# A four-layer convolution and pooling trunk on eight cores: another scratch buffer for the short convolution, half-size weight blocks, and matmuls placed over the joints

## The chip, the cores and the metric

One Trainium2 chip, all eight cores. Two sequences of 4096 tokens are cut into eight pieces of 1024, and each core works alone on its piece plus 92 tokens of history; nothing is exchanged. The time of a run is that of its slowest core, in microseconds (us) on the device.

A run comes in one of two states. In a *slow* run the cores of one die (0 to 3 or 4 to 7), sometimes of both, have a lower granted TensorE clock (the share of full speed that the throttle lets through, 1.00 at most) and take longer. I use *undisturbed cores*: the cores of a fast run at its highest clock. In the kernel before they differ by 20 us (5170 to 5190 in its profile), and so do their waits for weights (47 us on core 6, 63 on core 0).

## The reference, cut to what matters

```python
def conv_mixers(h, ...):                       # even layers
    a_val, a_gate, b_x, b_c, b_b = jnp.split(h @ w_in, ...)        # 5 x 1024 columns
    a = a_val * sigmoid(a_gate)                                    # GLU
    a = causal_depthwise_conv(a, conv_a_w) + conv_a_b              # 31 taps
    a = silu(layernorm(a, ...))                                    # over 1024 channels
    bo = b_b * causal_depthwise_conv(b_c * b_x, conv_b_w)          # 3 taps
    return concat([a, bo]) @ w_out
def reference(x, ...):
    for layer in range(4):
        h = rmsnorm(x, norm_mix_g[layer])
        x = x + (conv_mixers(h, ...) if layer % 2 == 0 else pool_mixer(h, ...))
        h = rmsnorm(x, norm_mlp_g[layer])
        x = x + square(relu(h @ w1)) @ w2                          # 2048 -> 8192 -> 2048
    return rmsnorm(x, final_g)
```

## The kernel before

Channels lie on the 128 partitions; a *column* is 128 channels, so mixers A and B have eight columns each. Tokens are cut into three tiles of up to 372. The engines are PE (TensorE, the matmuls), DVE (VectorE), ACT (ScalarE), POOL (GpSimd) and SP (SyncE); PSUM is the memory that PE's results go to, and the kernel uses eight banks of it. A small list scheduler in the program orders the instructions of DVE, ACT, POOL and SP by modelled readiness and priority; PE keeps program order. What a buffer's name says decides the dependencies: an instruction that writes a buffer waits for all earlier readers of it.

The 31-tap convolution of an A column is split by taps (one product of the input, shifted, with one coefficient): DVE does 22 taps in an accumulator in PSUM, ACT makes nine products and POOL adds them into one accumulator `pacc` through two scratch buffers, `prod`. The three-tap convolution of a B column uses the same two:

```python
q = cnt["prod"] % 2                            # conv(j), 31 taps; once per tap of POOL's share
P.act(... out=prod[q][:, o0:T], in_=a[:, o0 + kk:T + kk], scale=col(wb + kk) ...)
P.pool(... out=pa, in0=pa, in1=prod[q][:, o0:T], op=ALU.add ...)
# ... cut
q = cnt["prod"] % 2                            # B_mm, the short convolution; same two buffers
P.act(... out=prod[q][:, o0:T], in_=pbuf[:, o0 + kk:T + kk] ...)
P.pool(... out=cv[:, o0:T], in0=cv[:, o0:T], in1=prod[q][:, o0:T], op=ALU.add ...)
for (lo, hi) in ot:                            # at once after it: PE's third projection
    mm_item(bk, *bv, ...)                      # and DVE's product with cv, which frees the bank
    P.dve(... out=cb[:, 8 + j, lo:hi], in0=pst(bk, hi - lo), in1=cv[:, lo:hi], op=ALU.mult ...)
```

The mixer's order, the start of the program, and the joints (places where PE needs a norm):

```python
A_mm(0); A_mm(1); B_mm(0); A_mm(2); B_mm(1); A_mm(3); B_mm(2); B_mm(3)   # two columns each
# ... half of the output projection (B), then
for (lo, hi) in ot:
    ln_tile(lo, hi)                            # LayerNorm, tile by tile, PE has nothing else
# ... the other half of the output projection (A)
for (lo, hi) in split(0):                      # start: squares, norm, normed x, then projections
    for c in range(KC):
        square(c, lo, hi, "dve")
    to_normed(C_GMIX)(lo, hi)
even_mixer(0, to_raw(C_GMLP))
for (lo, hi) in split(M0[0]):                  # norm ahead of each MLP
    rms_row(lo, hi)
mlp(0, ...)
```

## Time and profile before

| | before |
|---|---|
| three timed runs | 5814, 5924, 5990 us (median 5924.39) |
| profiled run (fast) | 5190.0 us, mean clock 0.961 |
| PE busy / idle in it | 4713 / 477 us |
| first MLP matmul of layer 0 | 714.6 us |

The prediction below shows the lines that it rests on. The busy time by stretch of the kernel before, from the first projection to the LayerNorm (columns: stretch, its length, then busy time and instructions of PE, PE's weight loads, DVE, ACT and POOL, then granted clock, DMA share, GB/s):

```profile
84.70:608.80 524.10, 382.20 (x2304) 228.81 (x2303) 318.90 (x320) 147.36 (x170) 205.64 (x104) 0.87 0.28 49
```

PE has work for 382 of 524 us, and no other engine is full either. Then PE's timeline from the LayerNorm to the MLP (start, length, engine, source line, and in brackets the idle time before it and what ended it), and one joint of an odd layer:

```profile
608.85 1.39 PE L361 MATMUL ps<-cb,ones 128*128 128x362 bf16 x8
...
654.04 51.56 PE L361 MATMUL ps<-cb,wr 128*128 128x362 bf16 x320 [7.68 <-ACT cb L576]
705.43 1.38 PE L403 MATMUL ps<-scr,onesf 128*128 128x362 f32 x4
710.71 1.54 PE L403 MATMUL ps<-scr,onesf 128*128 128x362 f32 x2 [3.90 <-POOL scr L397]
714.58 5.80 PE L361 MATMUL ps<-hb,wr 128*128 128x362 bf16 x19 [2.32 <-DMA wr<-w]
...
1739.11 3.91 PE L403 MATMUL ps<-scr,onesf 128*128 128x358 f32 x6 [10.91 <-POOL scr L397]
```

The LayerNorm's first matmul is at 608.85, the MLP's at 714.58. At the joint (1739.11) PE waits 10.9 us for POOL's sums of squares.

### The profile page before, as it was taken

Reading aid. Unit: us, or ns where it says so; the run is one execution under the profiler, and the core shown is the slowest. Engines: PE = TensorE matmul, PEld = TensorE weight load, DVE = VectorE, ACT = ScalarE, POOL = GpSimd, SP = SyncE. Lnnn points to the kernel's source line nnn. Section 1 sums busy time; section 2 is a strip of 40 time slices with the busy share of each in tenths; the row PEclk is TensorE's granted clock in tenths of the full one; section 3 lists DMA queues with packets and bytes.
Section 4 is the critical chain, followed back from the end, with each engine's and each line's share of the span. In section 5 each row is a group of like instructions: output and inputs, shape, how many; then the busy total and the mean of one; then the engine's idle time right before and its main releaser. Section 6 shows DMA issues by size and latency. Waiting matters only on the chain.

```text
span 5190.0 us, 80534 instructions; the slowest of 8 cores (5169.9 to 5190.0 us)
## 1 busy us (share of the span) xinstructions
PE 4713.3 (91%) x31214; PEld 3023.5 (58%) x31214; DVE 1883.0 (36%) x2944; ACT 1119.8 (22%) x1998; POOL 863.1 (17%) x845
## 2 busy tenths in 40 slices
PE   3477899999999899999984788999999989999998
PEld 1244556666665566666652455666666656666665
DVE  5855432222233422222359555322222352222235
ACT  2322340101015501010123224301010271011012
POOL 1543030000003300000036441200000140000003
PEclk9788999999999999999997899999999999999999
DMA  5133333443342344444421323344434424444443
GB/s 114 18 53 62 57 59 73 74 74 70 70 73 51 65 74 74 74 74 74 74 44 31 65 49 66 68 77 77 74 74 76 76 46 75 81 74 75 80 74 98
DMA packets 59991, 354.67 MB, mean 68 GB/s; under 512 B 6112, under 2 KB 18528, under 8 KB 19680
## 3 DMA queue, kind: packets, MB, share of 16 engines
q0 software_dynamic: 46224, 331.58, 35.2%
q1 hardware_dynamic: 13392, 17.93, 1.1%
q8 instruction: 255, 4.18, 0.3%
q14 instruction: 120, 0.98, 0.1%
HBM read 672.66 MB, written 8.39 MB: 131 GB/s over the span
## 4 chain that ended last, share of the span: by engine, by line
PE 83%; DVE 5%; DMA 4%; POOL 3%; issue 2%; ACT 2%; DVEq 0%; POOLq 0%; ACTq 0%; SPq 0%
PE ps L361 81%; POOL scr L485 3%; DMA wr<-w_in 3%; DVE ps L490 2%; PE ps L632 1%; DVE hb L415 1%; DMA xs<-x 1%; PE ps L675 1%; DVE xs L420 0%; DVE xs L794 0%; PE ps L403 0%; DVE scr L397 0%; ACT scr L395 0%; DMA wr<-w 0%; POOL scr L397 0%
## 5 line engine op out<-in xcount | busy, mean ns | idle before, releaser
L361 PE MATMUL ps<-hb,wr 128*128 128x358 bf16 (+7 forms) x13056 | 2018.9, 318 | 267.3 <-DVE cb L528 198.7
L361 PEld LDWEIGHTS ps<-hb,wr 128*128 128x128 bf16 x13056 | 1282.4, 98 | 1002.1 <-issue 302.1
L361 PE MATMUL ps<-cb,wr 128*128 128x362 bf16 (+6 forms) x10752 | 1626.9, 314 | 48.9 <-ACT cb L576 21.0
L361 PEld LDWEIGHTS ps<-cb,wr 128*128 128x128 bf16 x10752 | 1049.1, 98 | 622.5 <-issue 56.2
L420 DVE TENSOR_TENSOR xs<-ps,xs 128x362 f32<-128x362 f32 (+6 forms) x1152 | 602.2, 524 | 1418.4 <-PE ps L361 1418.2
L721 ACT ACTIVATE cb<-scr 128x362 bf16<-128x362 f32 (+6 forms) x768 | 380.8, 496 | 3067.8 <-DVE scr L718 3067.8
L718 DVE SCALAR_TENSOR_TENSOR scr<-ps,rstd 128x362 f32<-128x362 f32 (+6 forms) x768 | 402.5, 524 | 1426.4 <-PE ps L361 1426.4
L356 POOL DMA_DIRECT2D wr<-w x192 | 101.9, 531 | 2521.4 <-PE ps L361 2417.0
L361 PE MATMUL ps<-cb,scr 128*128 128x362 bf16 (+4 forms) x3072 | 463.9, 312 | 0.0
L361 PE MATMUL ps<-hb,scr 128*128 128x362 bf16 (+3 forms) x3072 | 463.2, 312 | 0.0
L490 DVE SCALAR_TENSOR_TENSOR ps<-scr,cst_sb,ps 128x1086 f32<-128x1086 f32 (+1 forms) x336 | 446.2, 1328 | 30.8 <-DVE ps L490 0.9
L361 PEld LDWEIGHTS ps<-cb,scr 128*128 128x128 bf16 x3072 | 298.4, 97 | 159.6
L361 PEld LDWEIGHTS ps<-hb,scr 128*128 128x128 bf16 x3072 | 298.4, 97 | 159.6
L397 POOL TENSOR_TENSOR scr<-scr 128x368 f32<-128x368 f32 (+7 forms) x360 | 314.1, 879 | 231.1 <-ACT scr L395 219.3
L485 POOL TENSOR_TENSOR scr<-scr 128x1086 f32<-128x1086 f32 (+1 forms) x128 | 312.2, 2439 | 227.1 <-ACT scr L476 112.0
L395 ACT ACTIVATE scr<-xs 128x362 f32<-128x362 f32 (+11 forms) x405 | 196.1, 491 | 90.2 <-DVE xs L420 67.4
L411 ACT ACTIVATE hb<-xs,cst_sb 128x362 bf16<-128x362 f32 (+6 forms) x288 | 169.5, 589 | 56.5 <-DVE xs L420 52.7
L482 ACT ACTIVATE scr<-scr,cst_sb 128x1086 f32<-128x1086 f32 (+1 forms) x128 | 150.8, 1180 | 132.2 <-POOL scr L485 129.2
L356 POOL DMA_DIRECT2D scr<-w x64 | 34.0, 531 | 842.9 <-PE ps L361 798.2
L403 PE MATMUL ps<-scr,onesf 128*128 128x358 f32 (+7 forms) x42 | 25.1, 722 | 135.7 <-DVE scr L397 79.9
L403 PEld LDWEIGHTS ps<-scr,onesf 128*128 128x128 f32 x42 | 10.0, 274 | 143.7 <-issue 142.9
L523 POOL TENSOR_TENSOR scr<-scr 128x1086 f32<-128x1086 f32 (+1 forms) x32 | 66.1, 2065 | 65.0 <-ACT scr L520 61.7
(61 smaller groups left out, 1024.1 us busy)
## 6 DMA issues: line engine op xcount, KB each, us to landing
wr<-w POOLq DMA_DIRECT2D x192, 1024.0 KB, 7.9
scr<-w POOLq DMA_DIRECT2D x64, 1024.0 KB, 7.9
wr<-w_in POOLq DMA_DIRECT2D x40, 1024.0 KB, 10.8
wr<-w_out POOLq DMA_DIRECT2D x16, 1024.0 KB, 8.2
xs<-x SPq DMA_DIRECT2D x12, 744.0 KB, 15.2
y<-xs SPq DMA_DIRECT2D x32, 171.0 KB, 2.4
wr<-pool_w POOLq DMA_DIRECT2D x8, 512.0 KB, 5.1
y<-xs SPq DMA_DIRECT2D x16, 170.0 KB, 2.2
```

The source lines that it names most:

```text
L356: P.dma("pool", lambda h: h.dma_start(out=wslot[s][:, 0:n], in_=src), wsem[s], [], wb, 128 * n * 4)
L361: fns = [(lambda h, i=i, l=l, r=r: h.matmul(pst(bk, w), lhsT=l, rhs=r, start=(i == 0), stop=(i == last))) for i, (l, r) in enumerate(parts)]
L395: P.act(w, lambda h: h.activation(out=t[:, 0:w], in_=xs[:, c, lo:hi], func=AF.Square), R(X[c], lo, hi), [tb], prio)
L397: f(w, lambda h: h.tensor_tensor(out=acc[:, lo:hi], in0=acc[:, lo:hi], in1=t[:, 0:w], op=ALU.add), [tb] + R(B_acc, lo, hi), R(B_acc, lo, h ...
L411: P.act(hi - lo, lambda h: h.activation(out=hb[:, c, lo:hi], in_=xs[:, c, lo:hi], func=AF.Identity, scale=col(gcol)), R(X[c], lo, hi) + [B ...
L420: P.dve(hi - lo, lambda h: h.tensor_tensor(out=xs[:, m, lo:hi], in0=pst(bk, hi - lo), in1=xs[:, m, lo:hi], op=ALU.add), [PS[bk]] + R(X[m], ...
L482: P.act(L, lambda h, kk=kk, q=q: h.activation(out=prod[q][:, o0:T], in_=a[:, o0 + kk:T + kk], func=AF.Identity, scale=col(wb + kk)), ab + ...
L485: P.pool(L, lambda h, q=q: h.tensor_tensor(out=pa, in0=pa, in1=prod[q][:, o0:T], op=ALU.add), R(B_prod[q], o0, T) + pb, pb, 2)
L490: P.dve(L + 90, lambda h, kk=kk: h.scalar_tensor_tensor(out=cacc, in0=a[:, o0 + kk:T + kk], scalar=col(wb + kk), in1=cacc, op0=ALU.mult, o ...
L523: P.pool(L, lambda h, q=q: h.tensor_tensor(out=cv[:, o0:T], in0=cv[:, o0:T], in1=prod[q][:, o0:T], op=ALU.add), R(B_prod[q], o0, T) + R(B_ ...
L718: P.dve(w, lambda h, bk=bk, w=w, t=t, lo=lo, hi=hi: h.scalar_tensor_tensor(out=t[:, 0:w], in0=pst(bk, w), scalar=0.0, in1=rstd[:, lo:hi], ...
L721: P.act(w, lambda h, w=w, t=t, f=f, lo=lo, hi=hi: h.activation(out=cb[:, f, lo:hi], in_=t[:, 0:w], func=AF.Square), [tb], R(C[f], lo, hi), 0)
```

## The change

Its intent is to fill PE's holes outside the MLPs. Six parts:

1. **Scratch.** The short convolution uses `rstd`, idle during the mixer, in place of `prod`.
2. **Order.** Its last projection and product (`B_last`) come a step after the first part (`B_first`); columns go one by one.
3. **Half blocks.** The input projection is loaded in blocks of one column, in six half slots.
4. **Taps.** POOL and ACT take 11 of the 31 taps (9 before); ACT also starts DVE's accumulator.
5. **Start.** PE multiplies x before it is normed (gain only); rstd is applied to the results.
6. **Joints and LayerNorm.** Half of the output projection lies between the LayerNorm's tiles; the first MLP matmuls come ahead of the norm's row; the last norm of a tile comes after the next tile's first matmuls.

The diff holds more: the scheduler's modelled costs of POOL's work and of DMA issues are lower, weight slots are taken in another order, and some priorities and one late load differ.

```diff
-CONVP = 9
+CONVP = 11
-    win_d = nc.dram_tensor("w_in", [2, 20, 128, SLOT], ...)
+    win_d = nc.dram_tensor("w_in", [2, 40, 128, HALF], ...)
 # ... cut: load_h, six half slots; column-wise glu; raw start (start0)
+                P.act(L, lambda h: h.activation(out=cacc, in_=a[:, o0:T], func=AF.Identity, scale=col(wb)), ...)
-                P.dve(L, lambda h: h.tensor_scalar(out=cacc, in0=a[:, o0:T], scalar1=col(wb), ...), ...)
 # short convolution
-                        P.act(... out=prod[q][:, o0:T], in_=pbuf[:, o0 + kk:T + kk] ...)
-                        P.pool(... in0=cv[:, o0:T], in1=prod[q][:, o0:T] ...)
+                    P.act(... out=rstd[:, a:b], in_=pbuf[:, a + kk:b + kk] ...)
+                    P.pool(... in0=cv[:, a:b], in1=rstd[:, a:b] ...)
+            for j in (2, 4, 6):
+                A_mm(j)
+                A_mm(j + 1)
+                B_last(j - 2)
+                B_first(j - 1)
+                B_last(j - 1)
+                B_first(j)
 # LayerNorm
-            for (lo, hi) in ot:
-                ln_tile(lo, hi)
+            w = load_w(wout_d[i, 1, 2], SLOT)
+            ln_tile(*ot[0])
+            out_b(2, *w, (0, 1))
+            ln_tile(*ot[1])
+            out_b(2, *w, (2, 3))
+            w = load_w(wout_d[i, 1, 3], SLOT)
+            ln_tile(*ot[2])
+            out_b(3, *w)
 # odd layers' joint
+                            bks = [[w1_mm(wv, wb, mi, lo, hi) for mi in range(2)] for (lo, hi) in tiles]
+                            for bk2, (lo, hi) in zip(bks, tiles):
+                                rms_row(lo, hi)
-        odd_mixer(1, to_raw(C_GMLP + KC))
+        odd_mixer(1, to_raw(C_GMLP + KC, prio=0))
```

## The prediction

> **What bounds the kernel now.** I read the table of cores first, then the PE's waits, then stretches of the timeline, then the busy time by stretch.
>
> ```profile
> core 0: 5190.0 us, clock 0.961
> ...
> die 0 (median of its cores): 5177.6 us, clock 0.961
> die 1 (median of its cores): 5177.5 us, clock 0.961
> ```
> Both dies are equal, so the profiled execution (5190 us) was undisturbed. The timed runs (5814 to 5990 us, median 5924) were not like it: they are 734 us longer at the median. I work out the change on the profile and carry it to the timed runs at the end.
>
> ```profile
> PE ps L361 <- DVE cb L528: 201.1, 8, 65.6
> PE ps L403 <- DVE scr L397: 79.9, 3, 42.6
> PE ps L361 <- DMA wr<-w_in: 63.4, 19, 6.5
> PE ps L403 <- POOL scr L397: 55.8, 10, 10.9
> PE ps L361 <- ACT cb L576: 21.0, 3, 7.7
> PE ps L361 <- DVE cb L581: 19.5, 2, 9.8
> ```
> These are what TensorE (PE) waits for: total, times, longest. They sum to 441 us, nearly all of the 477 us in which PE is idle (5190 less 4713 busy). Line 528 is the last product of the short convolution, 397 the sum of squares of a norm, 576 and 581 the LayerNorm's output.
>
> ```profile
> core 0: us, PE busy (x) PEld busy (x) DVE busy (x) ACT busy (x) POOL busy (x), PEclk, DMA share, GB/s
> 0.00:84.70 84.70, 4.77 (x7) 1.81 (x8) 45.38 (x84) 24.33 (x51) 2.48 (x8) 1.00 0.62 152
> 178.00:256.00 78.00, 12.70 (x82) 7.71 (x80) 71.58 (x56) 25.14 (x22) 45.92 (x19) 0.61 0.00 0
> 256.00:504.00 248.00, 185.28 (x1088) 109.12 (x1088) 149.85 (x140) 73.05 (x78) 108.17 (x56) 0.88 0.32 57
> 614.00:654.00 40.00, 16.55 (x80) 8.81 (x78) 35.67 (x67) 28.04 (x45) 4.13 (x2) 0.72 0.07 15
> 714.00:1663.00 949.00, 945.95 (x6144) 594.55 (x6144) 232.44 (x433) 144.58 (x288) 73.95 (x108) 1.00 0.38 69
> ```
> The stretches are: start and first norm; the hole of the first even mixer; the rest of its projections; its LayerNorm; the first MLP. The MLP is full (946 of 949 us), so only the mixers, their joints and the two ends can give anything. The MLP also gives the price of a matmul: 945.95/6144 = 154.0 ns at 362 columns. In the 256-504 stretch no engine is full: DVE 60%, POOL 44%. So this is a chain of waits, not a full engine.
>
> ```profile
> 247.00 2.48 POOL L485 TENSOR_TENSOR scr<-scr 128x1086 f32<-128x1086 f32 x1 [0.20 <-POOL scr L485]
> 249.43 2.12 POOL L523 TENSOR_TENSOR scr<-scr 128x1086 f32<-128x1086 f32 x1
> ...
> 256.25 19.11 PE L361 MATMUL ps<-hb,wr 128*128 128x372 bf16 x112 [65.56 <-DVE cb L528]
> ```
> This is the largest wait. The first short convolution's POOL add (L523) stands after 32 adds of the long convolutions (L485, four convolutions of eight), because both use the two `prod` buffers in program order. PE has queued the products that need it, runs out of its five PSUM banks, and waits 65.6 us, later 19 and 19 (62, 16, 17 in layer 2).
>
> [...] the trace shows 0.61 and 0.88 granted in the stretches with holes, 1.00 in the MLP, so closing a hole also warms the matmuls after it. [...]
>
> **The change part by part.** Matmul counts of the projections do not change.
>
> *Start of layer 0.* Before, PE's first projection matmul is at 84.5 us: all x tiles and three 2.1 MB weight blocks (fp32 as read) share the DMA, the first x lands at 29.4 us, and each tile is squared, summed, normalised and scaled before PE starts. After, matmuls run on gain-scaled x and rstd is applied to their results; only one pair of half blocks (2.1 MB) precedes tile 0. The DMA delivered about 7.5 MB as read in the first 26 us (4.3 MB as written, of which 3.15 MB of weights count double), so some 290 GB/s. Tile 0 with its weights and constants (5.5 MB) is then in by about 21 us. Sixteen fp32 sums of squares on PE at 0.7 (warm, 1.38 for two at 705 us) to 1.6 us (cold, at 43 us) end near 35 us. The third pair of halves may land only near 55 us and hold PE some 10 us. The first block (two A columns and one C·x column, three tiles: 288 matmuls at 157.5 ns = 45 us) therefore ends near 97 us.
>
> *Middle.* Short convolutions use rstd as scratch, not `prod`, and their last product is emitted one step later (B_last), so that it is ready. I tested each engine on one pair of columns in layer 0. PE: 480 matmuls x 157.5 = 75.6 us. DVE: two convolutions of 19 taps (11 now go to ACT and POOL, one to ACT) and a last add, 40 x 1.457 (cadence of L490) = 58, plus 18 evacuations at 0.6 = 69 us; with 23 operations per convolution it would have been 78. POOL: 20 adds x 2.69 = 54, four short adds x 2.3 = 9, ten half loads at 0.55 = 68 us. ACT: 24 x 1.2 + 6 x 1.2 + 12 x 0.5 = 42 us. So PE is the bound, narrowly. The one accumulator of POOL makes a serial chain per convolution: first product 1.5 + ten adds 27 + loads and short adds between 7 + final DVE add 2 = 37.5 us, 75 us a pair: equal to PE. I leave 10 us of stall where the fourth column needs the first of three A buffers, 5 us at the end of the last convolution, 5 us for loads and cold clocks: 20 us of the 165 us of waits now between 84 and 654 us.
>
> *LayerNorm.* Its three tiles cost 23.5 us of PE waits (9.8, 6.0, 7.7). After, 192 matmuls of the other output half (29 us) are spread between and after them, and a tile's DVE chain is some 12 us, so they are hidden; DVE does 36 + 13 us in a stretch of 37 us and runs over by about as much as the second half of the projection gives.
>
> *Sum of layer 0*, to the first MLP matmul (714.6 us): 97 + 1632 x 157.5 ns (257) + 816 x 153.3 ns (125) + 20 + three norm matmuls 4.5 = 504. Saved: 210.
>
> *Layer 2*, from 2636.4 to 3282.9 (646.5 us): last two tiles of the MLP 39, projections 1920 x 151.7 = 291, output half and LayerNorm 816 x 147.5 = 120, six norm matmuls 9, waits 23: 482. Saved: 164. This holds the deferred norm of each tile, whose waits (5.3 and 7.0 us) go away.
>
> *Odd mixers.* Each ends with a wait for the squares (10.9 and 10.3 us). After, six groups of the MLP (14.8 us) come first: 20 saved. *End:* the finishes of tiles 0 and 1 move behind the next tile's first matmuls: 2.3 + 5.9 = 8 saved; the last 15 us stay.
>
> Together 210 + 164 + 20 + 8 = 402, so about 4790 us in the state of the profile, 0.92 of before.
>
> **Rivals.** *POOL becomes the bound.* It goes from 8 to 10 adds per convolution, gets the squares and rstd products of the start and twice as many loads, and stands in order: a load that waits for its slot holds up all adds behind it (POOL's waits for PE before a load are its longest). For it: 75 us of chain against 75.6 of PE, with nothing to spare. Against: half slots come free in half the time. If each of the eight convolutions ran 4 us late, each even layer would lose 30 us and the time in the profile's state would be 4850. *The clock takes it back.* [...] In the extreme nothing is gained (5900). Against: the clock was 1.00 throughout the full MLPs, so density alone did not throttle this execution. *Raw start fails.* If x tile 0 still lands near 30 us behind the weights, or the squares come in late, the first block ends near 120 us: 25 us lost, no sign changed. *The loads were the wait* (63 us on w_in): halves double the issues, but 1 MB landed in 8 to 11 us and half of it should take no longer, so I don't expect these waits to grow.
>
> **Range and chances.** In the timed runs PE is slower. Idle time that is removed does not scale, which gives 5924 - 402 = 5522. But the projections of the even layers, now dense (about 870 us of PE work), would stretch like the MLPs, by 16 to 23% or 140 to 200 us, of which the holes of the kernel before absorbed perhaps half: 70 to 100 us given back. At a slow clock POOL and DVE have slack, so the 20 us stalls shrink. I take 5580, a ratio of 0.942. The range 5400 to 5730 holds a mostly unthrottled spell at one end[...]. Faster by over 2%: 0.94; within: 0.05; slower: 0.01.
>
> **What would show it.** The first projection matmul near 35 us and the first full-width POOL add of a long convolution near 85; no PE wait over 12 us between 100 and 500 us; waits for the short convolution's product gone from 201 to under 20; granted clock over 0.95 there; the first MLP starting near 505; the LayerNorm's waits gone; MLP stretches unchanged to 1%. Wrong would be: PE waiting for the GLU products behind L516/L519 (the POOL chain), a first block that ends after 120 us, or MLPs at a lower clock than in before's run of the same state.

## The result, and the profile after

| | before | after |
|---|---|---|
| all runs up to the result | 15: median 5695, 5189 to 5996 | 14: median 4896, 4852 to 5649 |
| fast runs | from 5188.67 | seven, 4852 to 4862 |
| ratio of fast runs | | 0.9325 (95%: 0.9282 to 0.9368) |

A ratio here is the mean time of one kernel's fast runs over that of the other's fast runs of the same rounds, so it is not quite the ratio of medians or of profiled times. The change is faster by 6.7%. The predicted 5580 us, range 5400 to 5730, does not hold the measured 4896. That median is itself no typical run: it lies halfway between the slowest of seven fast runs (4862) and the fastest of seven slow ones (4931).

The profile recorded with the result fell in the slow state (first fence: its table of cores); a fast one (second fence) is the run called `a_same` below.

```profile
core 0: 5107.3 us, clock 0.924
...
core 4: 5503.8 us, clock 0.850
```

```profile
core 0: 4859.6 us, clock 0.980
core 1: 4860.2 us, clock 0.979
core 2: 4829.3 us, clock 0.987
...
core 4: 4832.6 us, clock 0.985
...
core 6: 4859.7 us, clock 0.979
```

Even in the fast run some pairs of cores (0 and 1, 6 and 7) end 27 us after the others. From about 2890 to 3050 us, around the start of MLP 2 (2925), their clock is 0.81. Two cores in the same 104 us:

```profile
core 1: us, PE busy (x) PEld busy (x) DVE busy (x) ACT busy (x) POOL busy (x), PEclk, DMA share, GB/s
2936.00:3040.00 104.00, 104.00 (x581) 63.51 (x580) 25.27 (x39) 21.79 (x43) 5.26 (x9) 0.81 0.39 62
...
core 2: us, PE busy (x) PEld busy (x) DVE busy (x) ACT busy (x) POOL busy (x), PEclk, DMA share, GB/s
2936.00:3040.00 104.00, 104.00 (x707) 68.60 (x706) 28.02 (x48) 23.90 (x49) 3.73 (x7) 1.00 0.39 72
```

Both are full of matmuls, but one gets through 581 and the other 707. So I compare stages on core 4, which has no dip. What PE waits for there (total, times, longest):

```profile
PE ps L372 <- DMA wr<-w_in: 14.8, 4, 11.3
PE ps L414 <- POOL scr L408: 14.3, 5, 4.2
PE ps L372 <- DVE cb L567: 14.2, 8, 3.3
PE ps L372 <- ACT cb L640: 13.5, 2, 7.0
PE ps L887 <- ACT scr L884: 13.3, 1, 13.3
PE ps L372 <- DVE scr L480: 10.9, 1, 10.9
```

Line 567 is now the short convolution's product: 14.2 us, against 201.1 before. Line 414 is the norm's row (55.8 before for POOL's squares), line 640 the LayerNorm's output, line 480 the GLU's product. The busy time by stretch: start and first block; rest of the projections; LayerNorm and output projection; first MLP.

```profile
core 4: us, PE busy (x) PEld busy (x) DVE busy (x) ACT busy (x) POOL busy (x), PEclk, DMA share, GB/s
0.00:114.00 114.00, 76.21 (x383) 42.79 (x384) 66.17 (x120) 45.42 (x78) 54.17 (x61) 0.90 0.64 140
114.00:412.00 298.00, 279.68 (x1778) 171.59 (x1776) 253.70 (x247) 158.79 (x181) 249.90 (x132) 0.98 0.45 66
412.00:523.00 111.00, 99.46 (x615) 60.85 (x614) 70.51 (x132) 71.08 (x129) 42.43 (x49) 0.92 0.42 66
523.00:1471.00 948.00, 945.10 (x6152) 594.25 (x6149) 238.39 (x436) 148.88 (x296) 77.54 (x112) 1.00 0.45 70
```

In the second row PE is at 94%, DVE at 85% and POOL at 84% of 298 us, at a clock of 0.98; before, PE had 73% (382.2 of 524.1) at 0.87. A matmul takes 157.3 ns here (279.68/1778), before 165.9 (382.20/2304). The MLP is unchanged: 945 us of matmuls. The stages side by side:

| stage | before | after | gain | predicted gain |
|---|---|---|---|---|
| start to layer 0's first MLP matmul | 714.6 | 523.05 | 191.5 | 210 |
| layer 0's MLP | 948.9 | 948.0 | 1 | 0 |
| layer 2: end of tile 0 of MLP 1 to MLP 2's first matmul | 649.0 | 482.0 | 167 | 164 |
| two odd joints | 94.1 + 92.5 | 94.8 + 92.2 | 0 | 20 |
| end | 68.2 | 68.2 | 0 | 8 |
| whole, undisturbed core | 5190.0 | 4832.6 | 357 | 402 |

The odd joints run from the mixer's first matmul to the end of the norm; the 96 MLP matmuls that now lie inside (14.8 and 14.2 us) are added on the side of before. The column before is its core 0, the slowest of eight cores that end between 5170 and 5190 us, so some 10 us of the 357 are a matter of which core one takes.

### The profile page after: what moved, and what is told of

It is laid out like the page before. It is cut to its first block, busy times and chain, and to the rows that moved or that the text cites. A ratio compares the mean times of both kernels' runs of the same rounds, so it can differ in the third digit from the quotient of the medians.

```text
span 5503.8 us, 80816 instructions; the slowest of 8 cores (5106.2 to 5503.8 us)
## 1 busy us (share of the span) xinstructions
PE 5371.3 (98%) x31236; PEld 3273.2 (59%) x31244; DVE 1815.7 (33%) x2905; ACT 1185.4 (22%) x2067; POOL 1014.8 (18%) x967
## 4 chain that ended last, share of the span: by engine, by line
PE 95%; DVE 2%; issue 1%; POOL 1%; ACT 0%; DMA 0%; SPq 0%; DVEq 0%; POOLq 0%; ACTq 0%
PE ps L372 92%; PE ps L703 1%; DVE ps L516 1%; PE ps L746 1%; DMA xs<-x 0%; POOL scr L880 0%; SPq L395 0%; DVE xs L752 0%; PE ps L414 0%; POOL scr L513 0%; POOL scr L550 0%; PE ps L676 0%; DVE xs L908 0%; DVE rstd L423 0%; DVE hb L437 0%
## 5 line engine op out<-in xcount | busy, mean ns | idle before, releaser
L372 PE MATMUL ps<-hb,wr 128*128 128x358 bf16 (+7 forms) x13056 | 2268.4, 344 | 46.2 <-ACT scr L879 11.6
L372 PEld LDWEIGHTS ps<-hb,wr 128*128 128x128 bf16 x13056 | 1374.9, 105 | 935.1 <-issue 62.3
L372 PE MATMUL ps<-cb,wr 128*128 128x362 bf16 (+6 forms) x10752 | 1866.7, 344 | 25.9 <-ACT cb L640 13.7
L372 PEld LDWEIGHTS ps<-cb,wr 128*128 128x128 bf16 x10752 | 1137.1, 106 | 748.2 <-issue 31.7
L372 PE MATMUL ps<-cb,scr 128*128 128x362 bf16 (+4 forms) x3072 | 540.9, 346 | 0.0
L372 PE MATMUL ps<-hb,scr 128*128 128x362 bf16 (+3 forms) x3072 | 537.9, 345 | 0.0
L406 ACT ACTIVATE scr<-xs 128x368 f32<-128x368 f32 (+7 forms) x360 | 171.7, 486 | 89.6 <-DVE xs L442 80.3
L703 PE MATMUL ps<-wr,hb 128*128 128x512 bf16 x280 | 79.9, 453 | 1.6 <-issue 0.9
L550 POOL TENSOR_TENSOR scr<-scr,rstd 128x1086 f32<-128x1086 f32 (+6 forms) x40 | 79.6, 1992 | 6.3 <-ACT rstd L547 4.2
L423 DVE RECIPROCAL rstd<-scr 128x358 f32<-128x358 f32 (+7 forms) x21 | 49.5, 2361 | 78.7 <-ACT scr L421 78.7
```

Source lines behind the costliest of these rows:

```text
L372: fns = [(lambda h, i=i, l=l, r=r: h.matmul(pst(bk, w), lhsT=l, rhs=r, start=(i == 0), stop=(i == last))) for i, (l, r) in enumerate(parts)]
L406: P.act(w, lambda h: h.activation(out=t[:, 0:w], in_=xs[:, c, lo:hi], func=AF.Square), R(X[c], lo, hi), [tb], prio)
L703: fns = [(lambda h, k=k, bk=bk, lo=lo, hi=hi, m=m: h.matmul(ps[0:m, bk * 512:(bk + 1) * 512], lhsT=hb[:, 4 * g + k, lo:hi], rhs=wv[:, k * ...
```

## The experiments

Thirteen runs follow, eleven edited kernels and the changed kernel twice, all correct. The theory: nearly all of the gain comes from the short convolution's wait, and the prediction's size went wrong only because it took the slow state for the usual one. Rivals: the gain comes from the start, the order, or the half blocks; or a denser kernel is throttled more. The record's verdict on the first three edits (scratch alone, `prod` back, no deferral) is "unclear", and three edits have too few fast runs for any; what follows rests on undisturbed cores and on the waits. The kernels were not all run on the same chip; the kernel before reads alike on all of them (5164 to 5194), and the changed kernel on two (4829 to 4836).

**The changed kernel again (`a_same`, and later `a_again`).** No edit.

> The changed kernel once more, for a trace in the fast state. Fast runs 4850 to 4865 us, ratio to the kernel before 0.93 to 0.94. Theory A (the chain of the short convolution was the main wait): PE's waits for the short convolution's product fall from 201 us to under 30 over both even layers, and the first MLP starts between 515 and 530 us instead of 714.6. Theory B (the weight loads were the main wait) would show PE waits for w_in gone (63 us before) but the product's waits still over 60 us. On the states: if slow runs come with the chip and not with the kernel, this kernel has slow runs about as often as the kernel before in these rounds; if a denser TensorE is throttled more, it has clearly more.

> The changed kernel on the same chip as the three runs before, for comparison: fast runs 4850 to 4865 us, undisturbed dies 4835 to 4850.

*Measured.* `a_same`: one fast run of five, 4861.7 us, others 5105 to 5715; no ratio. `a_again`: fast runs 4859 to 4863, ratio 0.936 (0.9342 to 0.9379); undisturbed cores 4829 to 4836. 15 of 26 runs of the changed kernel were slow; of the kernel before, 16 of 32 in the experiments and at least 9 of the 15 with the result. So a denser kernel is not in the slow state notably more often, and outside the short dips its MLPs stay at 1.00 in the fast state. The rival "the clock takes it back" finds no support here.

**The kernel before, with the short convolution's scratch alone changed.**

```diff
-  P.act(... out=prod[q][:, o0:T] ...);  P.pool(... in1=prod[q][:, o0:T] ...)
+  P.act(... out=rstd[:, o0:T] ...);     P.pool(... in1=rstd[:, o0:T] ...)
```

> The kernel before with one thing of the change: the short convolution's products go into rstd's buffer in place of the two prod buffers. Theory A: its POOL adds no longer stand behind 32 long-convolution adds, PE's waits for the product fall from 201 to under 80 us, and the time from 5190 to about 5070 (fast). Rival: the long convolution itself (three A buffers, 23 DVE steps of 1.46 us, 40 to 50 us per column behind the projections) takes its place as the wait, the time stays within 60 us of 5190.

*Measured.* 4999.8, 5000.4 and 5037.4 us in its fast runs, ratio to before 0.9637 (0.9576 to 0.9698); undisturbed cores 4978 to 4998, some 190 us below before. Its PE waits:

```profile
PE ps L403 <- DVE scr L397: 80.0, 3, 42.7
PE ps L361 <- DMA wr<-w_in: 65.7, 19, 7.1
PE ps L403 <- POOL scr L397: 57.9, 10, 13.5
...
PE ps L361 <- DVE cb L526: 14.4, 8, 4.8
```

The product's wait falls from 201.1 to 14.4 (line 526 here, 528 before), and the time by the same 190; the other waits stand as they were. One buffer's name gives over half of the whole gain.

**The changed kernel, with `prod` back.**

```diff
-  P.act(... out=rstd[:, a:b] ...);     P.pool(... in1=rstd[:, a:b] ...)
+  P.act(... out=prod[q][:, a:b] ...);  P.pool(... in1=prod[q][:, a:b] ...)
```

> The changed kernel with the scratch put back to the two prod buffers, all else kept (later last product, half slots, new start). Theory A: the waits for the product come back in part (20 adds stand ahead in place of 32, and the product is used 30 us of PE later), 60 us per even layer, about 4970 us. Rival (the later product alone is enough, the scratch does nothing): under 4880 us.

*Measured.* 5051 to 5077 us, ratio 0.9742 (0.9695 to 0.9789); undisturbed cores 5044 to 5050, so 210 us lost.

```profile
PE ps L372 <- DVE cb L569: 214.1, 8, 41.3
```

The wait is back whole (line 569 is the product), although `B_last` is deferred here. So the scratch alone gives 190 us, and without it 210 of some 345 are lost; the deferral does not hide a wait of this size.

**No deferral.**

```diff
             short_conv(0)
+            B_last(0)
             for j in (2, 4, 6):
                 A_mm(j)
                 A_mm(j + 1)
-                B_last(j - 2)
                 B_first(j - 1)
                 B_last(j - 1)
                 B_first(j)
-            B_last(6)
+                B_last(j)
```

> The changed kernel with each column's last product emitted right after its own C.x product, all else kept. Theory A: each of eight products per layer waits for three ACT passes and two POOL adds (some 10 us, less what the five banks buffer), 40 us per layer, about 4930 us. Rival (the free scratch alone is enough): within 15 us of 4853.

*Measured.* Fast runs 4848.5 to 4899.7 us, ratio 0.9371 (0.9277 to 0.9465); undisturbed cores 4840 to 4851: some 10 us lost. The product's wait is 26.3 in 13 instead of 14.2 in 8. My expectation of a large loss was a miss: with scratch of its own the short convolution is ready soon, and the deferral has little left to hide.

**LayerNorm not interleaved.**

```diff
-            w = load_w(wout_d[i, 1, 2], SLOT)
-            ln_tile(*ot[0]) ... out_b(3, *w)
+            out_b(2, *load_w(wout_d[i, 1, 2], SLOT))
+            out_b(3, *load_w(wout_d[i, 1, 3], SLOT))
+            for lo, hi in ot:
+                ln_tile(lo, hi)
```

> The changed kernel with the three LayerNorm tiles after all of the first output half, as in the kernel before, all else kept. The changed kernel still waits about 11 us per even layer in its LayerNorm (4.5 and 7.2 us) against 23.5 before, so if the interleaving is worth only the difference, this is 25 us slower: fast runs near 4878. If it is worth the whole LayerNorm as my prediction had it, 45 to 50 us slower: 4900.

*Measured.* 4893 to 4913 us, ratio 0.9434 (0.9393 to 0.9476); undisturbed cores 4872 to 4877: 40 us lost, two layers together.

```profile
PE ps L372 <- ACT cb L640: 61.9, 6, 16.9
```

The LayerNorm's wait is 61.9 in six instead of 13.5 in two: the interleaving does its work.

**The start of before, all else changed.**

```diff
-        even_mixer(0, to_raw(C_GMLP), start0)
+        for (lo, hi) in split(0):
+            for c in range(KC):
+                square(c, lo, hi, "dve")
+            to_normed(C_GMIX)(lo, hi)
+        even_mixer(0, to_raw(C_GMLP), lambda n, lo, hi: None)
```

> The changed kernel with the start of the kernel before: each x tile squared, summed and normalised before PE's first projection matmul at about 84.5 us, all else kept. By the traces the first block of 288 matmuls ends at 113 us in the changed kernel; here it would end at 84.5 + 45 = 130. So 15 to 20 us slower: fast runs near 4870. Rival (the raw start is worth the 58 us by which the first projection matmul came earlier): 4910.

*Measured.* 4842.5 to 4869.3 us, ratio 0.935 (0.9302 to 0.9397); undisturbed cores 4836 to 4841. The raw start, the longest part of the diff, is worth about 5 us, although PE's first projection comes at 26.5 us with it and at 78.1 without (84.7 in the kernel before). (The expectation's 113 us is a misreading: counted in the next fence, the first block's 288 matmuls end at about 105.) Where the gain stops is in the PE timeline of the changed kernel (core 4, second run of the same):

```profile
26.50 5.21 PE L372 MATMUL ps<-hb,wr 128*128 128x372 bf16 x32
...
50.80 6.47 PE L372 MATMUL ps<-hb,wr 128*128 128x372 bf16 x32 [11.26 <-DMA wr<-w_in]
...
102.22 32.92 PE L372 MATMUL ps<-hb,wr 128*128 128x372 bf16 x208 [0.97 <-DVE scr L473]
146.05 14.16 PE L372 MATMUL ps<-hb,wr 128*128 128x362 bf16 x81 [10.91 <-DVE scr L480]
...
410.42 1.39 PE L372 MATMUL ps<-cb,ones 128*128 128x362 bf16 x8 [2.80 <-DVE cb L519]
```

With the old start the LayerNorm's first matmul is 5.6 us later (core 0 of that run):

```profile
416.01 1.39 PE L372 MATMUL ps<-cb,ones 128*128 128x362 bf16 x8
```

Two chains of nearly the same length end there. With the old start PE sets the time: it is busy for 326 of the 332 us between 78.1 and 410.5. With the raw start PE is ahead and gives the time back, in the wait of 10.9 us for a free A buffer (line 480) and in 2.8 at the end, and the chain of convolutions sets the time: its eight column adds (line 519) lie 37.5 us apart on average, from 146.6 to 409.0 us. That chain does not begin sooner. DVE's first step of a long convolution is at 117.1 us with the raw start and at 116.4 with the old one, its last add at 409.0 and 410.6.

The timeline and kernel.py tell why, though no run tests it. The first column's input is there at 102.2 us, when ACT forms the first product from it, but the accumulator on DVE's side lies in the PSUM banks (5 to 7) in which the raw start keeps its copies of rstd, and DVE's normed tiles read these until 114.3; ACT opens the accumulator at 115.9. It is the shared scratch over again, in a new place.

**Nine taps in place of eleven.**

```diff
-CONVP = 11
+CONVP = 9
```

> The changed kernel with 9 in place of 11 taps of the long convolution on ACT and POOL. Theory A: DVE then needs 22 operations of 1.457 us per column, 75 us a pair with the evacuations, as much as PE, and stalls come: 10 to 30 us slower in all, 4865 to 4885. Rival (POOL's serial chain was the tighter one, and it is relieved): not slower, 4840 to 4855.

*Measured.* One fast run of four, 4910 us with a disturbed pair, so no ratio; undisturbed cores 4852 to 4864: 20 to 25 us lost. PE's wait for the column add (line 519) grows from 2.8 to this:

```profile
PE ps L372 <- DVE cb L519: 30.6, 2, 15.5
```

That fits the chain as the bound: with nine taps DVE's half of it is the longer one. In layer 0 the column add waits for POOL in five of eight columns with eleven taps and in none with nine, where DVE does the last nine steps of the last column back to back.

**Joints of before.** Norm rows ahead of the MLP, gains at the old priority, last norm not deferred.

```diff
+            for (lo, hi) in tiles:
+                rms_row(lo, hi)
-                    if gi == 0 and blk == 0:
+                    if False:
-                                if late and (blk, mi) == (0, 2):
-                                    late()
 # ... cut
+                        by_tile(lo, hi)
-        odd_mixer(1, to_raw(C_GMLP + KC, prio=0))
+        odd_mixer(1, to_raw(C_GMLP + KC))
```

> The changed kernel with all joints as before: norm rows ahead of the MLP's first matmuls, gains of the odd mixers at the old priority, tiles finished at once and not behind the next tile's first matmuls. By the stretches of the two traces the new joints gain nothing at the odd mixers and nothing at the end, some 6 us at each even mixer's end and some 10 us before layer 2: 20 to 25 us slower, 4875. Rival (my prediction: 20 at the odd mixers, 8 at the end, besides those): 50 us slower, 4905.

*Measured.* Two fast runs (4934.5, 4935.6), both with dips, too few for a ratio; undisturbed cores 4862 to 4866: 31 us lost.

```profile
PE ps L414 <- POOL scr L408: 56.9, 10, 12.2
```

The parts together are worth 31 us, but not where I put them: against this run's core 3, the changed kernel gains about 5 and 4 us at the ends of the even mixers, 13 before layer 2 and 4 at the end. At the odd joints the stage table shows no gain:

```profile
1538.33 16.28 PE L372 MATMUL ps<-hb,wr 128*128 128x358 bf16 x96 [2.53 <-ACT hb L428]
1557.79 2.47 PE L414 MATMUL ps<-scr,onesf 128*128 128x358 f32 x4 [3.17 <-POOL scr L408]
1564.56 1.52 PE L414 MATMUL ps<-scr,onesf 128*128 128x354 f32 x2 [4.30 <-DVE scr L788]
```

The one wait of 10.9 us has become three, 2.5, 3.2 and 4.3, with 96 matmuls between at 16.3 us, where 96 at the first MLP's 154.0 ns would take 14.8. With the joints of before, the norm's first matmul comes 75 to 77 us after the start of layer 1's mixer (cores 2 and 3); here 86.7. So the new order itself brings the squares some 10 us later, and the matmuls put ahead hide nothing. That the gains, now first in ACT's order, push the squares back is likely, but not separated from the rest. The third wait is of the order's own making: six MLP groups and three norms want nine of eight PSUM banks, and the third norm waits for DVE to empty one.

**Half slots four deep, not six.**

```diff
+            if cnt["h"] > 6:                   # a load also waits for the readers of the next two slots
+                more = W[(s + 1) % 6].r + W[(s + 2) % 6].r
+                P.ops[n].deps = sorted(set(P.ops[n].deps) | set(more))
```

> The changed kernel with each half-block load of the input projection held back until the two next older half slots are free too, so that four half slots work in place of six; nothing else changes. If the finer and earlier loads are a part of the gain (PE's waits for w_in are 63 to 66 us in the kernels with whole slots and 14 in the changed one), these waits come back to over 40 us and the time rises by 30 or more, 4885. If the order of the short convolution is all, the time stays within 10 us of 4853 and the waits for w_in under 25 us.

*Measured.* One fast run, 4864.9, no ratio; undisturbed cores 4829 to 4836, as with six. PE's waits for w_in are 17.6 us on core 6 (14.8 with six). Depth past four is worth nothing here.

**Odd joints: every second gain on DVE.**

```diff
-                gain(c, lo, hi, gbase + c, prio)
+                (gain_dve if prio == 0 and c % 2 else gain)(c, lo, hi, gbase + c, prio)   # tensor_scalar
```

> The changed kernel with every second gain of the odd mixers on DVE (0.41 us) in place of ACT (0.59 us). Theory C (the joint after an odd mixer hangs on ACT, which has 48 gains, 48 squares and 36 evacuations, 76 us in a stretch of 71): ACT loses 14 us per odd layer, the squares come earlier and the joint shortens by 5 to 10 us each, 10 to 20 us in all: 4835 to 4845. Rival (POOL's chain of adds or the last matmuls set it): within 5 us of 4853.

*Measured.* 4873.7 and 4874.1 us, ratio 0.9384 (0.9361 to 0.9406); undisturbed cores 4847: 14 us worse, a miss. The moved operation itself (minimum, median and longest in ns):

```profile
L848 DVE TENSOR_SCALAR hb<-xs,cst_sb x48: 365/561/4268, 1498.4 to 3916.9; 128x368 bf16<-128x368 f32 x16, 128x384 bf16<-128x384 f32 x16, 128x318 bf16<-128x318 f32 x8, 128x272 bf16<-128x272 f32 x8
```

I had counted 0.41 us each, the median of the start's gains on DVE (412 ns at 372 columns, line 869 of `a_same`). Half of them take 561 ns or more, and one takes 4.27 us and ends with POOL's row of adds beside it:

```profile
3909.49 4.27 DVE L848 TENSOR_SCALAR hb<-xs,cst_sb 128x272 bf16<-128x272 f32 x1
3909.91 3.69 POOL L408 TENSOR_TENSOR scr<-scr 128x272 f32<-128x272 f32 x5
```

So the operation spreads by twelve times (365 to 4268 ns), and its longest instance ends at 3913.76 us, 0.16 us after the last of five POOL adds. No run here separates whether the adds hold it up.

**Everything that looked promising together.** That gain split, one A column moved behind `B_last`, and the LayerNorm's tiles closer.

```diff
                 A_mm(j)
-                A_mm(j + 1)
                 B_last(j - 2)
                 B_first(j - 1)
+                A_mm(j + 1)
 ...
             ln_tile(*ot[0])
-            out_b(2, *w, (0, 1))
             ln_tile(*ot[1])
+            out_b(2, *w, (0, 1))
+            ln_tile(*ot[2])
             out_b(2, *w, (2, 3))
```

> An attempt at a better version: the gains of the run before this, the fourth A column moved behind a B column so that it no longer waits for the first convolution (10.9 us of PE wait), and the second LayerNorm tile pulled in front of the output matmuls. If the long convolutions' own chain (117 to 410 us in layer 0, 36.7 us per column) bounds the even mixers, the moved column gains nothing and the LayerNorm 5 us per layer at most: 4825 to 4845 with the gains. If PE's waits are what counts, 25 us more: 4810 to 4820.

*Measured.* 4873.9 to 4920 us, ratio 0.9415 (0.9363 to 0.9466); undisturbed cores 4849 to 4852: no better than the gain split alone.

```profile
PE ps L372 <- DVE cb L519: 30.2, 2, 17.0
```

The wait for an A buffer that the new order takes away comes back at the end of the chain, as a wait for the last column add. A chain that bounds a stage is not shortened by moving where one waits for it.

**The kernel before with scratch and half blocks.**

```diff
 # on top of the scratch edit
-    win_d = nc.dram_tensor("w_in", [2, 20, 128, SLOT], ...)
+    win_d = nc.dram_tensor("w_in", [2, 40, 128, HALF], ...)
+        def load_h(src): ...                   # six half slots
-                xv = load_w(win_d[i, 8 + r], SLOT)
+                    xv = load_h(win_d[i, 16 + j])
```

> The kernel before with the rstd scratch and, besides, the input projection's weights in 40 half blocks with six half slots in place of 20 whole ones with three slots; the order of the work, the start, the taps, the LayerNorm and the joints stay as in the kernel before. The kernel with the scratch alone takes 5000 us and still waits 66 us for w_in. If the finer loads are what the remaining difference hangs on, these waits fall under 20 us and the time to 4940 to 4960. If the convolutions' chain takes their place, the waits fall but the time stays above 4980.

*Measured.* 4983 and 5012.5 us, ratio 0.9596 (0.9489 to 0.9702). Most cores of the fast runs took 4978 to 4983 us at a clock of 0.970 to 0.972, but two took 4958 and 4959 at 0.976 and 0.977 (and two of a slow run 4955 and 4958). The profiled cores 0 to 3 are of the first kind and show dips (0.77 at 1560 to 1670 us, 0.79 at 3990 to 4110, where the scratch alone has 0.91 to 0.94 in like stretches). So the undisturbed time is about 4958, 20 to 40 us below the scratch alone (4978 to 4998). The 47 to 66 us of waits for the projection's weights are gone from its list, but another has grown (14 to 17 before; core 0):

```profile
PE ps L370 <- DVE cb L536: 39.1, 12, 6.9
```

So of the load waits, 22 to 25 us came back as a wait for the product, and the rest agrees with the gain. That load waits were in part on the path shows within one run too: in the kernel with the scratch alone, core 1 waits 47.2 us for weights and core 4 65.7, and core 4 ends 18.5 us later at nearly the same clock (0.979 and 0.978).

**The sum.** On undisturbed cores: scratch 190, halves 20 to 40, LayerNorm 40, joints 31, taps 20 to 25, deferral some 10, start 5. That is 316 to 341 of some 345 us (5167 to 5190 before, 4829 to 4836 after). The first two were added to the kernel before and the others taken from the changed one, so they need not add up; some 5 to 30 us stay unassigned, and the untested scheduler costs and slot order are where they may lie. "Nearly all of the gain" was too much for the scratch: it is somewhat over half.

## Why the prediction was right or wrong

**The bound and the main mechanism: right.** I named the product of the short convolution as the largest wait and the shared `prod` as its cause. Undone alone it costs 210 us, done alone it gives 190. This is shown by two runs from opposite sides.

**Layer 0, 210 predicted, 191.5 measured.** Two terms are mis-sized. "The first block ... therefore ends near 97 us": its 288 matmuls ended near 105. They began at 26.5 us (I had said 35), but took 54 us at a clock of 0.85 instead of 45 at 157.5 ns each, with 24.5 us of waits between them. And the stalls from there to the MLP, 20 predicted, were 29.9. The matmuls of that stretch were right: 386.5 us predicted with the norm's, 388.4 measured. The prices of a matmul that I used, 157.5, 153.3, 151.7 and 147.5 ns at 372, 362, 358 and 348 columns, are in the traces: 480 at 372 columns in 75.37 us and 1305 at 362 in 200 us (recorded slow profile of the changed kernel, core 4 before its clock falls), 288 at 358 in 43.71 and 288 at 348 in 42.48 us (kernel before). The signs I asked for: no wait above 12 us between 100 and 500 (10.9); the product's under 20 (14.2); clock over 0.95 (0.98, but 0.92 in the LayerNorm stretch); MLP at 523, not 505; the first full-width POOL add at 107, not 85.

**The rival "POOL becomes the bound": partly right.** I called the chain equal to PE, 37.5 us a column; the columns come every 37.5 us. It is why the raw start gives 5 us, and why moving columns gives nothing. "Raw start fails ... 25 us lost" was off in kind: it neither fails nor pays.

**LayerNorm "hidden": mostly.** Two waits of 4.5 and 7.05 us remain in layer 0.

**Layer 2, 164: right** (167), and in its terms: 459 us of matmuls and 23 of waits predicted, 457.7 and 24.3 measured.

**Joints, "20 saved", and end, "8 saved": wrong.** I took the waits to be covered by matmuls put ahead of them, and did not ask what the new order does to the squares: they come some 10 us later. The odd joints took 94.8 and 92.2 us, as before. At the end the first tiles' waits are shorter, but the stretch after the last norm matmul grew from 15.0 to 20.8 us; it is 19.0 with the joints of before too, so the new order is not the main cause of that, which stays open.

**The step that failed.** Up to "402, so about 4790 us in the state of the profile", the sum is 45 us too large, about 1% of the time (4832.6 on an undisturbed core, 4852 to 4862 for the slowest). What put the prediction outside its range is the step after: "In the timed runs PE is slower ... which gives 5924 - 402 = 5522 ... I take 5580". I carried the sum to the slow state because all three timed runs were slow, and the range left no room for fast ones. Of the stretch of "16 to 23%" that I gave the dense projections, the lower end is the excess over PE's busy time (734/4713); the upper was shown by no run then. The recorded slow profile has 21%: from 1000 to 1200 us, in the first MLP, core 7 at 0.81 gets through 1079 matmuls (185.4 ns each) and core 4 at 1.00 through 1305 (153.3). POOL and DVE do not stretch: before 600 us POOL's full-width add takes 2.49 us on core 7 and 2.50 on core 4, DVE's step 1.35 on both. With half of the runs slow, and if runs are independent, three slow ones in a row come up about one time in eight. For the slow state itself the step is fair: slow runs of the changed kernel cover 4931 to 5715 us, and the first three, all slow, took 5505 to 5649, inside the range. (That the predicted ratio of 0.942 equals that of the slowest run of each kernel, 5715 to 6062, is one pair of extremes and shows nothing.) As a ratio, the fast profile's 4790/5190 = 0.923 is no nearer to the measured 0.9325 than 0.942; it is the time that it would have placed, 4790 against 4852 to 4862.

In the recorded slow profile, cores 4 and 7 of the same die (clock is the third column from the right):

```profile
0.00:1300.00 1300.00, 1231.38 (x7825) 763.56 (x7826) 568.09 (x820) 364.43 (x562) 377.93 (x296) 0.98 0.42 76
1300.00:4050.00 2750.00, 2717.62 (x15189) 1631.55 (x15191) 860.29 (x1370) 565.62 (x982) 484.52 (x456) 0.81 0.33 59
4050.00:5500.00 1450.00, 1422.33 (x8227) 878.08 (x8228) 387.30 (x715) 255.37 (x523) 152.40 (x215) 0.80 0.33 63
```

```profile
0.00:1300.00 1300.00, 1245.46 (x6571) 721.01 (x6572) 525.88 (x738) 350.95 (x534) 371.10 (x283) 0.81 0.39 65
1300.00:4050.00 2750.00, 2718.45 (x15068) 1622.64 (x15067) 860.02 (x1366) 561.08 (x972) 482.72 (x454) 0.81 0.33 59
4050.00:5500.00 1450.00, 1410.73 (x9609) 931.43 (x9607) 433.53 (x801) 273.09 (x562) 159.27 (x230) 0.97 0.42 74
```

Core 4 is free for its first 1300 us (0.98) and at 0.81 and 0.80 to its end; core 7 is at 0.81 from its start for 4050 us and then free (0.97). Both are slow for about the same time, at opposite ends. The slow profile of the last experiment looks the same: core 4 at 0.80 in its last 670 us, core 6 at 0.84 and 0.79 in its first 900. A full PE does not bring it by itself: in two fast profiles (`a_same` and `a_again`) the first MLP, 948 us, is full at 1.00 in the records of all eight cores. What begins and ends the slow stretches is not shown: each core's record has its own zero, no run here moves the launch, and the short dips in the middle of fast runs are not explained either.

## What to carry to other kernels

When two chains share a scratch buffer, program order makes the urgent one queue behind the long one; look for an idle buffer before you reorder anything, for here that one name was worth more than all other parts together. Before filling a hole, ask which chain ends last at the far side of it: an earlier start or another order gives next to nothing if the next stage waits for a chain that begins no sooner. And before carrying a gain from a profile to timed runs, ask which state each was in, and give both states their share of the range.
